# Pooled features times group weights: three fp32r matmuls a group replaced by one plain fp32 matmul

## The chip, the cores and the metric

The kernel runs on one core of a Trainium2 chip. The metric is the device time of the whole program in microseconds (us), the median of several runs. A change of the time is read against the program before.

## The reference

The program computes one layer of a decoder trunk for 2048 prompt tokens and 64 sample tokens (8 sequences of 8), with a model width of 1024. Cut to what matters:

```python
h = rmsnorm(x, g_pre_mix)
q, k, v, u = split(h @ w_in)              # 512, 128, 128, 512 columns
attn = sink_attention(rope(q), rope(k), v)  # window 128, 8 heads, 2 kv heads
# pooling: 512 channels in 4 groups of 128, windows 2, 4, 8, 16
for g, w in enumerate((2, 4, 8, 16)):
    r = trailing_mean(u[:, g], w) - u[:, g]          # (tokens, 128)
    outs.append(r @ pool_w[g])                       # pool_w[g]: (128, 128)
pooled = concat(outs) * pool_scale
x = x + rmsnorm(concat(rmsnorm(attn), rmsnorm(pooled)) @ w_out)
x = x + rmsnorm(square(relu(rmsnorm(x) @ w_up)) @ w_down)
x = x + sigmoid(x @ w_ple_gate + b_ple_gate) * (p @ w_ple)
```

All inputs and outputs are float32. The change is in the product `r @ pool_w[g]` alone.

## The kernel before

The kernel keeps float32 accuracy with fp32r matmuls: an operand is split into a high part (a cast to fp32r) and a low part (the float32 value minus the high part), and `mm3` (L136 to L140) adds three products: high by high, high by low, low by high. `lo_of` (L134) makes the low part on VectorE.

The program is a chain of stages. The first one, up to about 425 us of the profile, goes through 17 tiles: tile -1 holds the 64 sample tokens, tiles 0 to 15 hold 128 prompt tokens each. Four generators make the work of a tile:

- `front(t)`: three gemms of the transposed input `hT` with `w_in`, eight chunks of the contraction by three matmuls each. `kvps` holds keys and values (256 columns), `qps` the queries (512), `ups` the pooling input u (512). Behind them come rotation (`rope`, VectorE and GpSimd, tiles `kr`, `qr`, `rb`) and the splits `khl`, `qhl`, which TensorE turns (`trk`, `trq`) into `kp`, `qT`.
- `attention(t)`: scores in `sc` (16 matmuls), a fused mask and maximum on VectorE (L514, into `pr` and `nm`), the exponential on ScalarE, the scaling of `pr` (L540, L542), 16 transposes `trp`, their split `pt`, and the product with the values, `po`; `part` and `mix` (L565, L566) collect it.
- `pooling(t)`: four transposes of u (`tru`) into `ux`, four levels of running sums on GpSimd (`us`), the pooled features `r` on VectorE (L607), their split `rr` (L620 and L134), and the product with the group weights, `pq` (L625): 4 groups of 3 matmuls with 128 moved columns (64 for tile -1). ScalarE copies `pq` into `mix` and squares it into `sq`.
- `finish(t)`: the sum of squares over channels by a plain fp32 matmul (`pss`, L637), and the store of `mix` to DRAM (`mixd`).

The group weights are loaded once by `load_pool_w`, multiplied by the scale (L335) and split into `pw` (L336 and L134). The attention of the sample tile (`scs`, `trps`, `pos`) uses plain fp32 matmuls.

`weave` writes the generators of neighbouring tiles into each other by fixed strings (`ORDER`, `ORDERW`, `ORDER1`, `ORDER2`); a planner then orders the instructions of each engine by a model of their times, so that an edit in one place moves rows in others. On the chip each engine works through its rows in that order. When the front of tile 15 has ended, its memory is given to the next stage, `Mixed`: weights `wo` and rows `mr` are loaded, `mr` is split into `ms` (ScalarE and L134), and the products `pab` begin, woven into the last tiles' attention. From there on the program goes through the mixing product, the feed-forward part and the gate.

The PSUM pools of the first stage are `scp` (scores), `tr` (transposes), `op` (`po`, `pq`, `pss`) and `mmp` (gemms), two buffers each.

Of the kernel before, what the change touches and what calls it, by code (L numbers as in the profile page):

```python
# [10 lines left out]
F32 = mybir.dt.float32  # L11
F32R = mybir.dt.float32r
BF16 = mybir.dt.bfloat16
AF = mybir.ActivationFunctionType
ALU = mybir.AluOpType
PSUM = bass.MemoryType.PSUM

P = 128
# [40 lines left out]
def tn(t):  # L59
    return NS if t < 0 else P  # L60
# [32 lines left out]
def trunk(ctx: ExitStack, tc: tile.TileContext, i: dict, o: dict):  # L93
    nc = tc.nc
    V, A, G, T, SY = nc.vector, nc.scalar, nc.gpsimd, nc.tensor, nc.sync
# [37 lines left out]
    def lo_of(out, full, hi, eng=V):  # L133
        eng.tensor_tensor(out=out, in0=full, in1=hi.bitcast(F32), op=ALU.subtract)  # L134

    def mm3(ps, lhs, rhs, first, last):  # L136

        T.matmul(ps, lhs[0], rhs[0], start=first, stop=False)  # L138
        T.matmul(ps, lhs[0], rhs[1], start=False, stop=False)  # L139
        T.matmul(ps, lhs[1], rhs[0], start=False, stop=last)  # L140
# [138 lines left out]
    with ExitStack() as sa:  # L279

        sw = sa.enter_context(ExitStack())
        wp = sw.enter_context(tc.tile_pool(name="wp", bufs=1, reuse_waits="tile"))
        fp = sw.enter_context(tc.tile_pool(name="fp", bufs=2, reuse_waits="tile"))
        ca = sa.enter_context(tc.tile_pool(name="ca", bufs=1, side="right", reuse_waits="tile"))
        pa = sa.enter_context(tc.tile_pool(name="pa", bufs=2, side="right", reuse_waits="tile"))
        scp = sa.enter_context(tc.tile_pool(name="scp", bufs=2, space=PSUM))
        tr = sa.enter_context(tc.tile_pool(name="tr", bufs=2, space=PSUM))
        op = sa.enter_context(tc.tile_pool(name="op", bufs=2, space=PSUM))
        mmp = sw.enter_context(tc.tile_pool(name="mmp", bufs=2, space=PSUM))

        queue(gains, i["gains_t"])

# [22 lines left out]
            V.tensor_scalar_mul(nssink, ssink, -1.0)  # L315

        wi = [wp.tile([P, 2, INC], F32R, name=f"wi{k}") for k in range(8)]
        pw = ca.tile([P, 2, 4, P], F32R, name="pw")

        def load_w_in(k, part):  # L320

# [8 lines left out]
        def load_pool_w():  # L330
            raw, sc = (over.pool.tile([P, 512], F32, tag="raw", bufs=9, name="raw", padded_shape=[P, 768]) for _ in range(2))
            pr = raw.rearrange("p (g d) -> p g d", g=4)
            SY.dma_start(pr, i["pool_w"][0].rearrange("g c d -> c g d"))
            SY.dma_start(sc, i["pool_scale"].to_broadcast([P, 512]))
            V.tensor_tensor(out=pr, in0=pr, in1=sc.rearrange("p (g d) -> p g d", g=4), op=ALU.mult)  # L335
            A.copy(out=pw[:, 0], in_=pr)  # L336
            lo_of(pw[:, 1], pr, pw[:, 0])

        vps = []
        for r in range(4):  # L340
# [230 lines left out]
        def pooling(t, u, mix, sq):  # L571

            n = tn(t)
            nb, w = (NDEC, TDEC) if t < 0 else (1, P)
            L = HALO + w
            ux = pa.tile([P, 4, nb, L], F32, tag="ux", bufs=2, name="ux", padded_shape=[P, 4, nb, 184 // nb])
            if t < 0:
                G.tensor_copy(ux[:, :, :, :HALO], past["u"].rearrange("p g (b j) -> p g b j", b=nb))
            elif t == 0:
                V.memset(ux[:, :, :, :HALO], 0.0)  # L580
            else:
                V.tensor_copy(ux[:, :, :, :HALO], state["ux"][:, :, :, P : P + HALO])
            ps = tr.tile([P, 4, P], F32, tag="tr", name="tru")
            for g in range(4):
                T.transpose(ps[:, g, :n], u[:n, g * P : (g + 1) * P], ident[:n, :n])
            A.copy(out=ux[:, :, :, HALO:], in_=ps[:, :, :n].rearrange("p g (b w) -> p g b w", b=nb))
            if t >= 0:
                state["ux"] = ux
            us = pa.tile([P, 2, 4, nb, L], F32, tag="us", bufs=1, name="us", padded_shape=[P, 2, 4, nb, 184 // nb])

            def m(ap, gs, a, b):
                v = ap[:, gs, :, a:b]
                return v.rearrange("p g b l -> p (g b) l") if nb > 1 else v[:, :, 0, :]

            for lev in range(4):
                d = 1 << lev
                src = ux if lev == 0 else us[:, (lev - 1) % 2]
                gs = slice(lev, 4)
                lo = 2 * d - 1
                G.tensor_tensor(  # L600
                    out=m(us[:, lev % 2], gs, lo, L), in0=m(src, gs, lo, L), in1=m(src, gs, lo - d, L - d), op=ALU.add
                )
            yield
            r = pa.tile([P, 4, P], F32, tag="r", bufs=1, name="r")
            for lev in range(4):
                s = us[:, lev % 2, lev]
                V.scalar_tensor_tensor(  # L607
                    out=r[:, lev, :n].rearrange("p (b w) -> p b w", b=nb),
                    in0=s[:, :, HALO:],
                    scalar=1.0 / (2 << lev),  # L610
                    in1=ux[:, lev, :, HALO:],
                    op0=ALU.mult,
                    op1=ALU.subtract,
                )
                if t == 0:
                    ic = ct[:, C_ICNT + lev * 16 : C_ICNT + (lev + 1) * 16]
                    V.tensor_tensor(out=r[:, lev, :16], in0=s[:, 0, HALO : HALO + 16], in1=ic, op=ALU.mult)
                    V.tensor_tensor(out=r[:, lev, :16], in0=r[:, lev, :16], in1=ux[:, lev, 0, HALO : HALO + 16], op=ALU.subtract)
            rr = pa.tile([P, 2, 4, P], F32R, tag="rr", bufs=1, name="rr")
            V.tensor_copy(rr[:, 0, :, :n], r[:, :, :n])  # L620
            lo_of(rr[:, 1, :, :n], r[:, :, :n], rr[:, 0, :, :n])
            yield
            pq = op.tile([P, 4, P], F32, tag="o", name="pq")
            for g in range(4):
                mm3(pq[:, g, :n], (pw[:, 0, g], pw[:, 1, g]), (rr[:, 0, g, :n], rr[:, 1, g, :n]), True, True)  # L625
            A.copy(out=mix[:, 4:8, :n], in_=pq[:, :, :n])
            A.activation(out=sq[:, 4:8, :n], in_=pq[:, :, :n], func=AF.Square)

# [155 lines left out]
        run(front(-1, *heads[-1], res[-1]))  # L784
        split_head(0)
        load_pool_w()

        last = iter(())
        for t in range(-1, NT):
            kr, vr, qr, u, kp, qT = res[t]  # L790
            if t + 1 < NT and t >= 0:
                split_head(t + 1)
            mix = pa.tile([P, 8, P], F32, tag="mix", bufs=2, name="mix")
            sq = pa.tile([P, 8, P], F32, tag="sq", bufs=2, name="sq")
            if t + 2 < NT:
                heads[t + 2] = head(t + 2)
            f = front(t + 1, *heads[t + 1], res[t + 1]) if t + 1 < NT else iter(())
            p = pooling(t, u, mix, sq)
            if t < 0:
                a = sample_attention(kr, vr, qr, mix, sq)  # L800
                for c in ORDER0.split():
                    next({"a": a, "p": p, "f": f}[c], None)
                run(a, p, finish(t, mix, sq))
                over_s.__exit__(None, None, None)
                over.pool = sa.enter_context(tc.tile_pool(name="over_p", bufs=1, side="right", reuse_waits="tile"))
                run(f)
            else:
                e = split_w_out((t - 3) % 4, (t - 3) // 4) if 3 <= t < 11 else iter(())
                if t == NT - 1:
                    sw.close()  # L810
                    s2 = ctx.enter_context(ExitStack())
                    mixed = Mixed(s2)
                    bank = sw.enter_context(tc.tile_pool(name="first", bufs=2, space=PSUM, reuse_waits="tile"))
                    e = mixed.first(bank)
                order = {NT - 2: ORDER1, NT - 1: ORDER2}.get(t, ORDERW if 3 <= t < 11 else ORDER)
                weave(order, a=attention(t, kp, qT, mix, sq), p=p, f=f, l=last, e=e)
                last = finish(t, mix, sq)
# [1094 lines left out]
```

## Time and profile before

| | |
|---|---|
| three runs | 2139.48, 2139.55, 2140.86 us; median 2139.55 |
| profiled execution | 2142.09 us, its span 2140.3 us |
| mean granted TensorE clock | 0.996 |
| TensorE busy, whole span | 2113.1 us (99%) |
| VectorE busy, whole span | 1622.4 us (76%) |
| product `pq`: rows of L138, L139, L140 | 68 each, median 273 to 275 ns |
| first and last product row | 51.8 and 419.0 us |

The span is the time from the first to the last instruction; the profiled execution's own time has 1.8 us around it and lies 2.5 us above the median of the runs. TensorE's busy time includes overlap of one matmul with the next, so that a busy engine alone does not tell how dense its work is: the distance between the starts of neighbouring rows does. PE is TensorE, PEld its weight loads, DVE VectorE, ACT ScalarE, POOL GpSimd, and SP issues the DMAs.

### The profile page before, as it was taken

The numbers are of one execution on the slowest core, as the hardware profiler recorded it, in microseconds if no ns is written. First come the engines' busy times: TensorE is split into PE (matmuls) and PEld (weight loads), VectorE is DVE, ScalarE is ACT, GpSimd is POOL, SyncE is SP. The second block draws the span as 40 slices with busy tenths as digits, with TensorE's granted clock in tenths as the row PEclk, the third lists the DMA queues.
The fourth block names the chain that finished last, engine by engine and source line by source line (L and its number), as shares of the span: only waits on it lengthen the run. The fifth ranks groups of instructions, "written<-read, shape, count | busy, mean of one in ns | idle before, by whom it ended". The sixth has DMA issues, their size and how long they took to land.

```text
span 2140.3 us, 31614 instructions
## 1 busy us (share of the span) xinstructions
PE 2113.1 (99%) x11343; PEld 1863.1 (87%) x11343; DVE 1622.4 (76%) x2794; ACT 1033.0 (48%) x2019; POOL 647.8 (30%) x689
## 2 busy tenths in 40 slices
PE   8999999999999999999999999999999999999999
PEld 6888888788889999999999998888888888887787
DVE  6899888876689888755555467778888888896786
ACT  4667666544555546454554445523323323233553
POOL 2334434343451110100000004644443443432242
PEclk9999999999999999999999999999999999999999
DMA  6552222768789989986776663223123123248563
GB/s 221 177 178 84 72 62 75 266 214 234 243 245 311 310 289 339 282 258 199 223 229 202 211 206 112 79 91 122 50 91 101 50 92 101 90 154 333 188 192 124
DMA packets 334107, 379.77 MB, mean 177 GB/s; under 512 B 82239, under 2 KB 263807, under 8 KB 323678
## 3 DMA queue, kind: packets, MB, share of 16 engines
q1 hardware_dynamic: 333950, 377.76, 55.4%
q8 instruction: 89, 1.46, 0.3%
q14 instruction: 68, 0.56, 0.1%
HBM read 247.90 MB, written 131.09 MB: 177 GB/s over the span
## 4 chain that ended last, share of the span: by engine, by line
PE 79%; DVE 7%; DMA 5%; issue 3%; POOL 3%; ACT 2%; SPq 0%; ACTq 0%; POOLq 0%; DVEq 0%
PE up L1142 9%; PE up L1144 9%; PE up L1143 9%; PE dn L1426 9%; PE dn L1428 9%; PE dn L1427 9%; PE pg L1663 2%; PE pg L1665 2%; PE pg L1664 2%; PE ups L138 1%; PE ups L140 1%; PE ups L139 1%; PE qps L140 1%; PE qps L138 1%; PE qps L139 1%
## 5 line engine op out<-in xcount | busy, mean ns | idle before, releaser
L1436 DVE TENSOR_TENSOR z<-dn,z 128x512 f32<-128x512 f32 x416 | 279.6, 684 | 89.6 <-PE dn L1428 83.6
L134 DVE TENSOR_TENSOR g<-raw,g 128x512 fp32r<-128x512 f32 x336 | 234.5, 716 | 99.7 <-ACT g L211 86.2
L1142 PE MATMUL up<-e,g 128*128 128x352 f32 x832 | 268.6, 324 | 4.0 <-ACT snap L1149 3.9
L1143 PE MATMUL up<-e,g 128*128 128x352 f32 x832 | 268.0, 322 | 0.0
L1144 PE MATMUL up<-e,g 128*128 128x352 f32 x832 | 265.1, 323 | 1.2 <-DVE g L134 1.2
L211 ACT CAST g<-raw 128x512 fp32r<-128x512 f32 x336 | 203.5, 622 | 88.4 <-PE up L1144 65.6
L1375 POOL TENSOR_TENSOR raws<-raws 128x1024 f32<-128x1024 f32 x32 | 80.3, 2512 | 429.1 <-DVE r L1157 376.6
L1426 PE MATMUL dn<-wr,ms 128*128 128x512 f32 x512 | 199.3, 390 | 0.4 <-DVE z L1436 0.4
L1427 PE MATMUL dn<-wr,ms 128*128 128x512 f32 x512 | 199.2, 389 | 0.0
L1428 PE MATMUL dn<-wr,ms 128*128 128x512 f32 x512 | 198.0, 389 | 0.0
L1142 PEld LDWEIGHTS up<-e,g 128*128 128x128 f32 x832 | 156.5, 188 | 6.2 <-ACT snap L1149 5.3
L1143 PEld LDWEIGHTS up<-e,g 128*128 128x128 f32 x832 | 157.3, 189 | 0.7
L1144 PEld LDWEIGHTS up<-e,g 128*128 128x128 f32 x832 | 156.2, 189 | 1.8 <-DVE g L134 1.8
L211 ACT CAST m<-fr 128x512 fp32r<-128x512 f32 (+1 forms) x128 | 65.4, 514 | 180.7 <-PE dn L1428 154.5
L856 POOL TENSOR_TENSOR s<-fr 128x256 f32<-128x256 f32 x64 | 49.1, 767 | 333.2 <-DVE ms L134 245.1
L1426 PE MATMUL dn<-wr,m 128*128 128x512 f32 x384 | 149.7, 390 | 0.2 <-ACT zp L1484 0.2
L1428 PE MATMUL dn<-wr,m 128*128 128x512 f32 x384 | 149.5, 389 | 0.0
L1427 PE MATMUL dn<-wr,m 128*128 128x512 f32 x384 | 149.4, 389 | 0.0
L1156 DVE TENSOR_TENSOR t<-up,snap 128x352 f32<-128x352 f32 x144 | 71.3, 520 | 78.8 <-ACT snap L1149 65.9
L1149 ACT COPY snap<-up 128x352 f32<-128x352 f32 x144 | 62.2, 454 | 136.3 <-PE up L1144 136.0
L1426 PEld LDWEIGHTS dn<-wr,ms 128*128 128x128 f32 x512 | 96.1, 188 | 20.6 <-DVE z L1436 0.6
L1428 PEld LDWEIGHTS dn<-wr,ms 128*128 128x128 f32 x512 | 96.1, 188 | 20.0
(382 smaller groups left out, 5862.5 us busy)
## 6 DMA issues: line engine op xcount, KB each, us to landing
raw<-in_w_up_dram SPq DMA_DIRECT2D x160, 256.0 KB, 4.8
raw<-upt SPq DMA_DIRECT2D x32, 1024.0 KB, 8.1
fr<-ffd SPq DMA_DIRECT2D x64, 512.0 KB, 3.6
ffd<-r SPq DMA_DIRECT2D x96, 256.0 KB, 2.6
upt<-raw SPq DMA_DIRECT2D x16, 1024.0 KB, 5.2
raws<-in_w_down_dram SPq DMA_DIRECT2D x32, 512.0 KB, 5.4
sp<-hfd SPq DMA_DIRECT2D x21, 704.0 KB, 6.4
gwd<-gw SPq DMA_DIRECT2D x28, 512.0 KB, 5.4
```

The costliest lines, as they stand in the source:

```text
L134: eng.tensor_tensor(out=out, in0=full, in1=hi.bitcast(F32), op=ALU.subtract)
L211: copy(out=dst[:, 0], in_=src)
L1142: T.matmul(ps, l[0], r[0], start=st, stop=False, skip_group_check=not fresh)
L1143: T.matmul(ps, l[0], r[1], start=False, stop=False, skip_group_check=not fresh)
L1144: T.matmul(ps, l[1], r[0], start=False, stop=c == 3, skip_group_check=not fresh)
L1149: A.copy(out=s, in_=ps)
L1156: V.tensor_tensor(out=t, in0=ps, in1=s, op=ALU.add)
L1375: tc.keep_in_program_order(G.tensor_tensor(out=t, in0=x, in1=y, op=ALU.subtract))
L1426: T.matmul(ps, l[0], r[0], start=fresh and j == 0, stop=False, skip_group_check=not fresh)
L1427: T.matmul(ps, l[0], r[1], start=False, stop=False, skip_group_check=not fresh)
L1428: T.matmul(ps, l[1], r[0], start=False, stop=j == 1, skip_group_check=not fresh)
L1436: V.tensor_tensor(out=z, in0=ps, in1=z, op=ALU.add)
```

## The change

The group weights are kept as one float32 tile `pw`, written by the product with the scale itself. The pooled features `r` are not split. Each group's product is one plain fp32 matmul. The four PSUM pools of the stage are given the rule `reuse_waits="tile"`, which the other pools have already.

```diff
-        scp = sa.enter_context(tc.tile_pool(name="scp", bufs=2, space=PSUM))
-        tr = sa.enter_context(tc.tile_pool(name="tr", bufs=2, space=PSUM))
-        op = sa.enter_context(tc.tile_pool(name="op", bufs=2, space=PSUM))
-        mmp = sw.enter_context(tc.tile_pool(name="mmp", bufs=2, space=PSUM))
+        scp = sa.enter_context(tc.tile_pool(name="scp", bufs=2, space=PSUM, reuse_waits="tile"))
+        tr = sa.enter_context(tc.tile_pool(name="tr", bufs=2, space=PSUM, reuse_waits="tile"))
+        op = sa.enter_context(tc.tile_pool(name="op", bufs=2, space=PSUM, reuse_waits="tile"))
+        mmp = sw.enter_context(tc.tile_pool(name="mmp", bufs=2, space=PSUM, reuse_waits="tile"))
...
-        pw = ca.tile([P, 2, 4, P], F32R, name="pw")
+        pw = ca.tile([P, 4, P], F32, name="pw")
...
-            V.tensor_tensor(out=pr, in0=pr, in1=sc.rearrange("p (g d) -> p g d", g=4), op=ALU.mult)
-            A.copy(out=pw[:, 0], in_=pr)
-            lo_of(pw[:, 1], pr, pw[:, 0])
+            V.tensor_tensor(out=pw, in0=pr, in1=sc.rearrange("p (g d) -> p g d", g=4), op=ALU.mult)
...
-            rr = pa.tile([P, 2, 4, P], F32R, tag="rr", bufs=1, name="rr")
-            V.tensor_copy(rr[:, 0, :, :n], r[:, :, :n])
-            lo_of(rr[:, 1, :, :n], r[:, :, :n], rr[:, 0, :, :n])
             yield
             pq = op.tile([P, 4, P], F32, tag="o", name="pq")
             for g in range(4):
-                mm3(pq[:, g, :n], (pw[:, 0, g], pw[:, 1, g]), (rr[:, 0, g, :n], rr[:, 1, g, :n]), True, True)
+                T.matmul(pq[:, g, :n], pw[:, g], r[:, g, :n], start=True, stop=True)
```

Behind the edit the code's lines stand up to five lines higher, so L625 becomes L620, L562 becomes L560, and so on. The rule on the PSUM pools changes no row's place on any engine and none of its waits; the rows move by the other edits.

The first place is TensorE's order at the product of tile 6, in the middle of the stage. `vp_136` and `vp_138` are the values of two key blocks, `wi_131` and `wi_132` the last two chunks of `w_in`. Before:

```order
L563 MATMUL po<-pt,vp_138 128x512
L475 MATMUL trq<-identr,qhl 128x128 x4
L138 MATMUL pq<-rr,pw 128x128
L140 MATMUL qps<-wi_131,hT 128x512
L138 MATMUL qps<-wi_132,hT 128x512
L139 MATMUL qps<-wi_132,hT 128x512
L140 MATMUL qps<-wi_132,hT 128x512
L139 MATMUL pq<-rr,pw 128x128
```

After the change, the same product:

```order
L560 MATMUL po<-pt,vp_136 128x512
L620 MATMUL pq<-r,pw 128x128 x2
L561 MATMUL po<-pt,vp_136 128x512
L560 MATMUL po<-pt,vp_138 128x512
L561 MATMUL po<-pt,vp_138 128x512
L473 MATMUL trq<-identr,qhl 128x128 x8
L620 MATMUL pq<-r,pw 128x128 x2
L138 MATMUL ups<-wi_129,hT 128x512
```

Before, ten more rows of the product follow; the product stands at the end of the query gemm. After, it stands inside the gemm for u, the next one of the front: the front is half a gemm and more further ahead of the pooling.

The second place is TensorE's order behind the front of tile 15, the last gemm of the stage, up to the first `pab`. Before, the part where TensorE waits (24 score matmuls stand behind the last gemm row in all, 32 `trp`, 8 `trq`):

```order
L511 MATMUL sc<-kp,qT 128x256
L585 MATMUL tru<-ident,u 128x128 x4
L552 MATMUL trp<-ident,pr 128x128 x8
L464 MATMUL trk<-identr,khl 128x128 x4
L475 MATMUL trq<-identr,qhl 128x128 x8
L552 MATMUL trp<-ident,pr 128x128
L510 MATMUL sc<-kp,qT 128x256
```

After (32 score matmuls, 40 `trp` and 16 `trq` behind the last gemm row), the end of this part:

```order
L561 MATMUL po<-pt,vp_136 128x512
L550 MATMUL trp<-ident,pr 128x128 x8
L462 MATMUL trk<-identr,khl 128x128 x4
L632 MATMUL pss<-small,sq 128x1 x2
L560 MATMUL po<-pt,vp_136 128x512
L561 MATMUL po<-pt,vp_136 128x512
L560 MATMUL po<-pt,vp_138 128x512
L473 MATMUL trq<-identr,qhl 128x128 x4
L561 MATMUL po<-pt,vp_138 128x512
L473 MATMUL trq<-identr,qhl 128x128 x4
L138 MATMUL pab<-wo,ms 128x512
```

The first `pab` now comes ahead of the last tile's scores, and more of the attention stands behind the front.

The third place is VectorE's order ahead of the first split of mixed rows (`ms`), between the last rotation of queries and `ms`. Before, the last of 71 instructions:

```order
L134 TENSOR_TENSOR pt<-trp,pt 128x512
L566 TENSOR_TENSOR mix<-po,part 64x512
L537 RECIPROCAL es<-es 128x4
L514 ISA pr,nm<-sc,ct,nsink 128x256
L514 ISA nm 128x1
L134 TENSOR_TENSOR ms<-mr,ms 128x1024
```

After, the last of 53:

```order
L605 SCALAR_TENSOR_TENSOR r<-us,ux 128x128
L134 TENSOR_TENSOR pt<-trp,pt 128x512
L605 SCALAR_TENSOR_TENSOR r<-us,ux 128x128
L134 TENSOR_TENSOR pt<-trp,pt 128x512
L634 TENSOR_SCALAR ss_4922<-pss 128x2
L134 TENSOR_TENSOR ms<-mr,ms 128x1024
```

The split has moved ahead of eight score reductions of the last tile, and the `rr` rows are gone.

## Prediction

> **What bounds the kernel now.** I read the page first for the share of each engine, then a table of stretches to find the bound of the stage that the change touches, then the waits of TensorE, and last the timeline of single instructions for prices. From the page, busy time by engine; from the table of stretches, its heading and four stretches (matmul, weight load, VectorE, ScalarE, GpSimd, then the granted clock, the DMA share and GB/s):
>
> ```profile
> PE 2113.1 (99%) x11343; PEld 1863.1 (87%) x11343; DVE 1622.4 (76%) x2794; ACT 1033.0 (48%) x2019; POOL 647.8 (30%) x689
> ...
> core 0: us, PE busy (x) PEld busy (x) DVE busy (x) ACT busy (x) POOL busy (x), PEclk, DMA share, GB/s
> 36.00:40.00 4.00, 4.00 (x12) 3.18 (x12) 3.53 (x15) 3.57 (x11) 2.75 (x6) 0.59 0.41 105
> ...
> 224.00:248.00 24.00, 24.00 (x151) 21.26 (x150) 22.91 (x65) 16.27 (x44) 9.00 (x12) 1.00 0.23 70
> ...
> 392.00:400.00 8.00, 6.32 (x41) 5.84 (x40) 7.17 (x23) 6.25 (x20) 4.02 (x6) 0.79 1.02 426
> 400.00:408.00 8.00, 7.17 (x41) 5.95 (x40) 7.91 (x19) 6.77 (x18) 4.00 (x4) 1.00 1.00 370
> ```
>
> The change lives in the first stage (0 to about 425 us). Its middle has TensorE busy 24.00 of 24.00 us at full clock, VectorE at 22.9. "Busy" is modelled at the end of a matmul, so I asked for the waits. TensorE's whole list between 60 and 440 us has six rows, first and last here, 4.9 us in all:
>
> ```profile
> PE trk L464 <- DVE pt L134: 1.3, 1, 1.3
> ...
> PE po L563 <- DVE pt L134: 0.4, 2, 0.2
> ```
>
> Every one but 0.2 us of these falls after 385 us. So from 60 to 385 us TensorE is fed without a break, and a microsecond of TensorE's work removed there is a microsecond of the program. Behind the stage the next one carries on with the same engine full, so what is gained is kept. Between 385 and 415 us it is otherwise: there VectorE is full and TensorE waits for it. These are the first matmul rows behind a wait, one early and five late (start, length, what, and in brackets the idle time and its releaser):
>
> ```profile
> 42.20 0.30 PE L721 MATMUL trps<-ident,prs 128*128 128x128 f32 x1 [0.67 <-DVE prs L717]
> ...
> 389.69 0.66 PE L552 MATMUL trp<-ident,pr 128*128 128x128 f32 x4 [0.71 <-ACT ux L586]
> 391.68 0.54 PE L464 MATMUL trk<-identr,khl 128*128 128x128 f32 x4 [1.34 <-DVE pt L134]
> 392.88 0.88 PE L475 MATMUL trq<-identr,qhl 128*128 128x128 f32 x8 [0.66 <-DVE pt L134]
> 394.79 0.45 PE L552 MATMUL trp<-ident,pr 128*128 128x128 f32 x1 [1.02 <-DVE pr L542]
> ...
> 404.94 0.50 PE L140 MATMUL pab<-wo,ms 128*128 128x512 f32 x1 [0.83 <-DVE ms L134]
> ```
>
> **The change, part by part: TensorE.** Removed are 12 fp32r matmuls a tile, three for each of four groups. A busy time does not tell what one of them costs, because they overlap; the distance from start to start does. One tile's product from its third matmul to the next gemm row, and for comparison two neighbours of 256 moved columns:
>
> ```profile
> 196.71 0.28 PE L140 MATMUL pq<-rr,pw 128*128 128x128 f32 x1
> ...
> 197.71 0.27 PE L140 MATMUL pq<-rr,pw 128*128 128x128 f32 x1
> 197.82 0.45 PE L140 MATMUL ups<-wi,hT 128*128 128x512 f32 x1
> ...
> 186.02 0.28 PE L139 MATMUL kvps<-wi,hT 128*128 128x256 f32 x1
> 186.14 0.28 PE L140 MATMUL kvps<-wi,hT 128*128 128x256 f32 x1
> ```
>
> Ten steps in 197.82 - 196.71 = 1.11 us: 0.111 us each, 12 x 0.111 = 1.33 us a tile. That is as much as a matmul of twice the columns nearly (186.14 - 186.02 = 0.12), so these short ones are held by their weight loads and not by the columns they move.
>
> Added are 4 plain fp32 matmuls a tile. The trace has plain fp32 only in the sample group's attention and in the sum of squares, never in this shape. Rows from there, and one fp32r row of 512 columns:
>
> ```profile
> L730 PE MATMUL pos<-ptn,vr x4: 376/402/427, 48.6 to 50.5; 64*64 64x256 f32 x4
> L733 PE MATMUL pos<-pts,sv x32: 222/223/243, 49.2 to 51.7; 128*64 128x32 f32 x32
> ...
> 179.07 0.40 PE L140 MATMUL ups<-wi,hT 128*128 128x512 f32 x1
> ...
> 32.59 0.43 PE L689 MATMUL scs<-kn,qTs 64*128 64x64 f32 x2
> 32.95 0.42 PE L682 MATMUL scs<-kT,qTs 64*32 64x128 f32 x8
> ```
>
> L733 issues 16 matmuls and stands in the trace 32 times, so one plain fp32 matmul is two records. L730 moves 256 columns and one record of it takes 376 to 427 ns, as an fp32r matmul of 512 does (0.40 us, row of 179.07): a record streams its columns twice. At 128 columns a record should then cost what 256 fp32r columns cost, 0.12 us, and a matmul 2 x 0.12 = 0.24. Below, it cannot go under two weight loads, 2 x 0.111 = 0.22. Above, the worst row is the lone L689, 32.95 - 32.59 = 0.36 us from its start to the next row's, an idle load queue included. I take 0.24, since the new ones stand in a dense stream like the kvps rows: 4 x 0.24 = 0.96 us a tile. Gain 1.33 - 0.96 = 0.37 us a tile (ends: 0.44 at 0.22; at 0.36 a loss of 0.11). Sixteen prompt tiles: 5.9 us. The sample tile moves 64 columns, so both kinds are held by loads: 12 x 0.111 - 8 x 0.111 = 0.44 us. TensorE together: 6.4 us, with ends of 7.5 and of -1.7 (16 x -0.11).
>
> The Trainium skill (TensorE: Matmul & The Clock Gate, Back-to-back issue gap) has a sustained 81 ns for a stream of load and matmul at 128 columns. By that the old product would be 12 x 81 = 0.97 us, as dear as the new one, and the sum would lose its main term. Here the same pair takes 0.111 us over ten steps, so the measurement decides against it.
>
> **VectorE and ScalarE.** The split of the pooled features into high and low goes, as does that of the group weights; the product with the scale stays, one row as before. Groups that write rr and pw (count, then ns least/median/most):
>
> ```profile
> L620 DVE CAST rr<-r x17: 275/418/1409, 46.2 to 410.4; 128x512 fp32r<-128x512 f32 x16, 128x256 fp32r<-128x256 f32 x1
> L134 DVE TENSOR_TENSOR rr<-r,rr x17: 404/683/1193, 47.1 to 412.9; 128x512 fp32r<-128x512 f32 x16, 128x256 fp32r<-128x256 f32 x1
> L336 ACT CAST pw<-raw x1: 617/617/617, 34.2 to 34.2; 128x512 fp32r<-128x512 f32 x1
> L134 DVE TENSOR_TENSOR pw<-raw,pw x1: 1327/1327/1327, 36.0 to 36.0; 128x512 fp32r<-128x512 f32 x1
> ```
>
> That is 17 x (0.42 + 0.68) = 18.7 us of VectorE. In the middle of the stage it is worth nothing, since TensorE, full there, covers VectorE. The weights' 1.33 us at 36.0 stands in VectorE's queue ahead of the softmax scaling (L717) that the transpose at 42.20 waits for: with it gone I take that wait as gone, 0.7 us (between 0, if the rotated queries ahead of it are late anyway, and 0.8 with the restart).
>
> What is late next: the pooled features r have one buffer and are now read by TensorE itself, where before VectorE copied them at once. VectorE's r of the next tile therefore waits for the product of this one, and behind it in VectorE's queue are exponent sums and the splits of probabilities. Even at the crowded end of the stage the trace has some 5 us from a product's last row to the next tile's r:
>
> ```profile
> 386.60 0.27 PE L140 MATMUL pq<-rr,pw 128*128 128x128 f32 x1
> ...
> 391.55 0.47 DVE L607 SCALAR_TENSOR_TENSOR r<-us,ux 128x128 f32<-128x128 f32 x1
> ```
>
> So I cost that wait at nothing. The reuse rule named on the four PSUM pools moves no row and no wait in the orders, so it costs nothing and gains nothing.
>
> **The moved rows.** With fewer splits to wait for, the order lets the front's gemms run further ahead: the product of tile 6 stands among the u gemm's rows, not the query gemm's. At the end of the front more attention is therefore left over: behind the last ups row stand 32 score matmuls, 40 transposes of probabilities and 16 of queries, where there were 24, 32 and 8. VectorE's side of the end is this (the last rotation of queries, the first split of mixed rows, the last mix):
>
> ```profile
> 377.33 0.75 DVE L414 TENSOR_TENSOR rb<-qps,cs 128x256 f32<-128x256 f32 x2
> ...
> 403.22 1.67 DVE L134 TENSOR_TENSOR ms<-mr,ms 128x1024 fp32r<-128x1024 f32 x1
> ...
> 424.70 0.69 DVE L566 TENSOR_TENSOR mix<-po,part 64x512 f32<-64x512 f32 x1
> ```
>
> The first pab rows, which fill TensorE again, need ms. Between the last rb and ms VectorE has 26 us of work in 71 instructions; in the new order 53 (8 score reductions and a pair of rr fewer). So ms comes earlier relative to the front's end, but the trp and po rows that stand ahead of the first pab need almost all of those 53 too. TensorE has some 10 us of its own work between the front's end and the first pab in both orders, and waits for the rest in both. I take the waits of the end as unchanged, 4.6 us with the five rows above; how far they can move is the main uncertainty. No DMA is added or removed; the loads of wo follow the front's end as before, one store of mix rows slips behind four loads of w_up, and nobody in this stage reads it.
>
> **The sum.** 6.4 + 0.7 = 7.1 us. The profiled execution takes 2142.09 us (span 2140.3 and 1.8 around it), so 2135.0. The three timed runs have their median 2.5 us lower, at 2139.55, and the forecast for such a median is 2139.55 - 7.1 = 2132.4. Runs agree within about 0.1%; 0.2%, 4.3 us, is what a measurement of this kernel can tell from no change.
>
> **Rivals.**
> *The end eats it.* If VectorE sets the end of the stage, the program gains only what VectorE gains there. Now it needs 425.4 - 377.3 = 48.1 us from the last rotation to the last mix. The new order takes out two rr pairs (2.2 us) and puts in what slid behind the front, roughly the VectorE share of 8 score matmuls, 8 transposes and a pooling (8 reductions, 2 splits and the rest, about 7 us by the rows' durations), so 53, and starts some 8 us earlier: the last mix 3 us earlier than now. Gain 3 us, 2136.6. For it: VectorE 7.91 of 8 at 400 to 408. Against: pab matmuls fill TensorE during that time, and TensorE has its own 6 us less.
>
> *The price is wrong.* At 0.36 us a matmul TensorE gains nothing: -1.3 + 0.7 gives 2140.1, no change. For it only a lone row with idle in it; against it the L730 record. By the skill's 81 ns the removed rows would be worth only 0.97 us a tile and the time be 2138.6; the ten measured steps leave that no chance of its own.
>
> *The end gains.* If the shorter VectorE queue takes the waits at 389.69 to 404.94 away, the lowered clock behind them goes as well (0.79 over 8 us: 1.7 us lost). Four rows of the chain that ended last, 2.0 us, are removed work and speak for it, the first and the last here:
>
> ```profile
> 397.02 0.34 DVE rr L620
> ...
> 412.93 0.60 DVE rr L134
> ```
>
> Then 7.1 + 4.6 + 1.7 = 13.4 in full, 2126.2; I expect at most half of the two, 10.2 in all: 2129.3 and a little below.
>
> *Slower.* At the end the new order puts trp x8 of the last tile but one ahead of the first pab, and the probabilities they read stand far down VectorE's queue, about 16 us behind the last rotation, where TensorE has 7 us of its own work after the front. A wait there of over 7.1 us more than today's 4.6 decides it, some 12 us in one place, after which the clock falls to half and costs again, as it does at 36 to 40 (granted 0.59):
>
> ```profile
> 35.97 0.63 PE L138 MATMUL qps<-wi,hT 128*128 128x512 f32 x1
> 36.40 0.63 PE L139 MATMUL qps<-wi,hT 128*128 128x512 f32 x1
> ...
> 39.33 0.39 PE L140 MATMUL qps<-wi,hT 128*128 128x512 f32 x1
> 39.56 0.40 PE L138 MATMUL qps<-wi,hT 128*128 128x512 f32 x1
> ```
>
> There the gemm's rows step by 0.43 us for 3.4 us, and by 0.23 after. A wait grown from 4.6 to 13.4 us (8.8 more) and half speed once more for 3.4 us (1.7) give 2132.4 + 10.5 = 2142.9. The Trainium skill (TensorE: Matmul & The Clock Gate, Part 1: The HAM clock gate) says that the clock halves after an idle window of about 3.4 us; the trace shows slow stretches of that length, here without a long idle time ahead of them.
>
> **How the numbers follow.** Forecast as summed, 2130 to 2135.2: 0.47. The end gains: 0.14. The end eats it: 0.21. Price wrong: 0.09. Slower: 0.09. Faster by over 0.2% (below 2135.2) are the first two and 0.02 of the third, whose near edge crosses that line: 0.63. Within 0.2%, the rest of the third and the fourth: 0.28. Slower: 0.09. The range runs from 2127.5 (price 0.22, 1.1 us more, with over half of the end's waits gone) to 2139.5 (price wrong), and leaves about 0.17 out.
>
> **What would show it.** The new product's rows should step by 0.24 us a matmul, in two records each; nothing else should be on rr; 60 to 380 us should stay without TensorE waits, with the u gemm of the last tile ending 8 to 9 us earlier, of which 6 are gain and 3 slid behind; the transpose near 42 us should not wait; the waits between the front's end and the first pab should add up to 4 to 6 us. The forecast is wrong if the records step by more than 0.15 us, if waits appear in the middle of the stage, or if those of the end grow beyond 8 us.

## The result, and the profile after

The changed kernel is slower: 2153.57 us median (2150.88 to 2156.89, 4 runs) against 2139.52 (4 runs) for the kernel before on the same chip, a ratio of 1.0057 [1.0045, 1.0069] (in brackets the 95% interval), 14 us more where 7 fewer were forecast. The profiled execution took 2154.9 us, its span 2152.8 us, with a mean granted clock of 0.992 (0.996 before).

The page's row of busy times is nearly unchanged, so the time is not in more work:

```profile
PE 2111.2 (98%) x11275; PEld 1859.2 (86%) x11275; DVE 1614.4 (75%) x2759; ACT 1033.9 (48%) x2018; POOL 642.4 (30%) x689
```

The table of stretches (columns as in the prediction) has the four stretches shown of before, and three new ones that are not full:

```profile
core 0: us, PE busy (x) PEld busy (x) DVE busy (x) ACT busy (x) POOL busy (x), PEclk, DMA share, GB/s
36.00:40.00 4.00, 4.00 (x12) 3.13 (x12) 3.21 (x15) 3.43 (x11) 2.90 (x6) 0.60 0.44 117
104.00:128.00 24.00, 22.53 (x140) 19.47 (x139) 21.26 (x59) 17.16 (x44) 9.50 (x13) 1.00 0.60 192
...
176.00:200.00 24.00, 22.29 (x140) 19.36 (x139) 21.80 (x61) 15.87 (x42) 10.72 (x13) 1.00 0.23 70
224.00:248.00 24.00, 24.00 (x151) 21.13 (x150) 20.13 (x59) 16.30 (x43) 9.26 (x13) 1.00 0.22 70
...
392.00:400.00 8.00, 6.51 (x26) 5.36 (x26) 5.64 (x11) 5.04 (x9) 1.07 (x2) 0.50 1.01 405
400.00:408.00 8.00, 8.00 (x43) 6.78 (x42) 3.20 (x12) 3.25 (x8) 0.00 (x0) 0.94 0.89 292
416.00:440.00 24.00, 18.36 (x89) 15.05 (x88) 14.22 (x27) 9.16 (x18) 6.60 (x9) 0.90 0.37 119
```

At 400 to 408 us VectorE, 7.91 of 8 us busy before, is down to 3.20: it now waits, as TensorE does at 416 to 440. TensorE's whole list of waits between 60 and 440 us (what waited, for whom, us in total, times, longest) had 4.9 us before and has 16.8:

```profile
PE pss L632 <- POOL sq L628: 5.6, 1, 5.6
PE trp L550 <- DVE pr L540: 4.8, 2, 4.1
PE ups L138 <- DVE vp L435: 1.5, 1, 1.5
PE trk L462 <- DVE pt L134: 1.5, 1, 1.5
PE po L561 <- DVE pt L134: 1.4, 3, 1.0
PE trq L473 <- DVE pt L134: 1.3, 1, 1.3
PE po L560 <- ACT pt L552: 0.7, 2, 0.3
```

Where they stand, by TensorE's timeline (start, length, row, idle time and releaser): three of the seven in the middle of the stage, then the end. The early wait at 42.20 us of before is gone.

```profile
123.31 0.54 PE L473 MATMUL trq<-identr,qhl 128*128 128x128 f32 x4 [1.34 <-DVE pt L134]
...
171.88 0.50 PE L561 MATMUL po<-pt,vp 128*128 128x512 f32 x1 [0.98 <-DVE pt L134]
...
195.00 0.47 PE L138 MATMUL ups<-wi,hT 128*128 128x512 f32 x1 [1.54 <-DVE vp L435]
...
389.68 0.52 PE L550 MATMUL trp<-ident,pr 128*128 128x128 f32 x3 [4.14 <-DVE pr L540]
...
393.68 0.75 PE L462 MATMUL trk<-identr,khl 128*128 128x128 f32 x4 [1.49 <-DVE pt L134]
...
437.50 1.02 PE L632 MATMUL pss<-small,sq 128*128 128x1 f32 x4 [5.57 <-POOL sq L628]
```

The wait for `pss` ends a chain of the last tile on three engines, here from ScalarE's and GpSimd's timelines, and VectorE had stood idle for that tile's transposes:

```profile
405.08 0.69 DVE L134 TENSOR_TENSOR pt<-trp,pt 128x512 fp32r<-128x512 f32 x1 [4.80 <-ACT pt L552]
...
434.67 0.63 ACT L567 ACTIVATE sq<-mix 128x512 f32<-128x512 f32 x1 [2.58 <-DVE mix L564]
...
435.38 1.26 POOL L627 TENSOR_TENSOR sq<-sq 128x512 f32<-128x512 f32 x1 [12.46 <-ACT sq L567]
```

The orders explain it. Before, 60 of the first 96 `pab` rows stood ahead of the last tile's last `po`, so 36 rows (8 us) were left to cover the chain from `po` to `pss`, which took 4.7 us (423.55 to 428.24). Now all 96 stand ahead of it, and nothing covers the chain. The last `po` and the `pss` of before, without a wait, and the last `po` now:

```profile
423.55 0.39 PE L563 MATMUL po<-pt,vp 128*128 128x512 f32 x1
...
431.99 0.50 PE L637 MATMUL pss<-small,sq 128*128 128x1 f32 x4
```

```profile
431.54 0.40 PE L561 MATMUL po<-pt,vp 128*128 128x512 f32 x1
```

Behind the long waits TensorE runs at half clock (granted 0.50 at 392 to 400): `pab` rows 0.43 us apart, where they are 0.23 apart a microsecond later.

```profile
399.81 0.63 PE L140 MATMUL pab<-wo,ms 128*128 128x512 f32 x1
400.24 0.63 PE L138 MATMUL pab<-wo,ms 128*128 128x512 f32 x1
...
401.54 0.40 PE L139 MATMUL pab<-wo,ms 128*128 128x512 f32 x1
401.77 0.39 PE L140 MATMUL pab<-wo,ms 128*128 128x512 f32 x1
```

The product itself is cheaper than forecast: four matmuls became 136 records over 17 tiles, two each (the group of the product's rows: count, ns least/median/most, first and last start):

```profile
L620 PE MATMUL pq<-r,pw x136: 270/275/345, 51.3 to 425.2; 128*128 128x128 f32 x128, 128*128 128x64 f32 x8
```

By the timeline four records ahead of a gemm row take 199.80 - 199.37 = 0.43 us, 0.11 each:

```profile
199.37 0.68 PE L620 MATMUL pq<-r,pw 128*128 128x128 f32 x4
199.80 0.47 PE L139 MATMUL ups<-wi,hT 128*128 128x512 f32 x1
```

Still the last u gemm row of tile 15 starts 6.2 us earlier than before (378.3 against 384.5 us), and the last product row 6.2 us later (425.2 against 419.0).

### The profile page after: what moved, and what is told of

It is laid out like the page before. It is cut to its first block, busy times and chain, and to the rows that moved or that the text cites. A ratio compares the mean times of both kernels' runs of the same rounds, so it can differ in the third digit from the quotient of the medians.

```text
span 2152.8 us, 31431 instructions
## 1 busy us (share of the span) xinstructions
PE 2111.2 (98%) x11275; PEld 1859.2 (86%) x11275; DVE 1614.4 (75%) x2759; ACT 1033.9 (48%) x2018; POOL 642.4 (30%) x689
## 4 chain that ended last, share of the span: by engine, by line
PE 79%; DVE 7%; DMA 5%; issue 3%; POOL 3%; ACT 2%; SPq 0%; ACTq 0%; DVEq 0%; POOLq 0%
PE dn L1421 9%; PE dn L1423 9%; PE dn L1422 9%; PE up L1137 9%; PE up L1139 9%; PE up L1138 9%; PE pg L1658 2%; PE pg L1660 2%; PE pg L1659 2%; DMA sp<-hfd 1%; PE ups L138 1%; PE ups L139 1%; PE ups L140 1%; PE qps L138 1%; PE qps L140 1%
```

## The experiments

The leading theory: the new product gains what TensorE saves, and the rows that the planner moved lose three times that. The experiments hold rows in a chosen order by edges that set the issue order on one engine and add no wait. Orders are given in words below, in place of the tables `ROWS`. All were timed against the kernel before on their own chip; ratios compare these. "97th pab" is the start of that row in the profiled execution, the point where the mixing stage has left the first one behind (held kernel before: 434.1).

| run | ratio to the kernel before | 97th pab, us | span, us |
|---|---|---|---|
| kernel before, order held | 1.0004 [0.9993, 1.0014] | 434.1 | 2142.8 |
| changed kernel | 1.0057 [1.0045, 1.0069] | 438.4 | 2152.8 |
| new product, old order | 0.9990 [0.9979, 1.0000] | 422.1 | 2138.3 |
| old product, new order | 1.0110 [1.0096, 1.0124] | 447.6 | 2158.4 |
| new order to tile 11, then old | 1.0012 [1.0002, 1.0023] | 432.3 | 2145.7 |
| old to tile 11, then new | 1.0049 [1.0037, 1.0061] | 435.0 | 2150.1 |
| old to tile 15, then new | 1.0034 [1.0023, 1.0045] | 433.0 | 2147.6 |
| old to the first pab, then new | 1.0023 [1.0012, 1.0034] | 431.9 | 2146.9 |
| 96 pab rows held behind attention | 1.0017 [1.0008, 1.0025] | 431.5 | 2143.3 |
| front rows held as well | 0.9996 [0.9988, 1.0005] | 424.8 | 2138.8 |
| product three times, old order | 1.0119 [1.0100, 1.0139] | 456.0 | 2167.2 |
| u gemm shorter, old order | 0.9939 [0.9926, 0.9953] | 417.1 | 2130.4 |
| copy ahead of cast, old order | 0.9991 [0.9980, 1.0001] | 422.9 | 2137.8 |
| loads ahead of store, old order | 0.9983 [0.9974, 0.9992] | 421.8 | 2135.4 |

**The new product in the old order.** `ROWS` holds every engine's rows of the kernel before, as runs of their places in the code.

```diff
+def keep_order(tc, nc):
...
+        for p, q in zip(seq, seq[1:]):
+            tc.add_manual_dep(
+                q,
+                p.name,
+                mybir.DependencyInfo(mybir.DependencyClass.NoSync, mybir.DependencyReason.DATA),
+                reason="keep_order",
+            )
...
         trunk(tc, ins, outs)
+        keep_order(tc, nc)
```

> The changed kernel's program, with every engine's rows held in the order that they have in the kernel before (edges of issue order alone, no wait added; the four matmuls stand where the first of each group's three stood). Theory A, the planner's moved rows cost and the product itself gains: 17 x (12 x 0.111 - 8 x 0.111) = 7.5 us off 2139.5, so 2132 us; no TensorE wait over 1 us between 104 and 200 us, the last tile's finish as late against its own rows as before. Theory B, the product itself makes the waits (TensorE now reads the one buffer of r, so VectorE's next tile waits for it): at least 2150 us in the old order too. Theory C, a gain on TensorE ahead of the end is given back at the end whatever the order: about 2139.5 us.

Measured 2139.07 us median, 0.9990: 14 us better than the changed kernel, so theory B falls, and the order is shown to cost what the changed kernel lost. The number is the one that theory C names, not the 2132 us of theory A; the next runs part these two. TensorE's waits between 60 and 440 us are down to six of 3.9 us, the longest two here:

```profile
PE trk L462 <- DVE pt L134: 1.3, 1, 1.3
PE trp L550 <- ACT ux L584: 0.7, 1, 0.7
```

But the 7.5 us do not show at the end as theory A has it: the mixing stage is 10 to 12 us ahead at the 97th pab (422.1 against 432.4 and 434.1 in the two profiles of the old program), and the median 0.9 us lower than that of the kernel before, by the interval 0 to 4.5. Not all of that lead is the product's: 3.2 and 4.9 us of it stand already at 59 us, where both profiles of the old program have half clock (granted 0.66 at 35 to 40 us, 0.79 and 0.57 at 52 to 60) and this one has none. The 7.1 us by which it grows from there are what 16 tiles should give, 16 x 4 x 0.111. Why less than that shows at the end is taken up below.

**The old product in the new order.** The kernel before, `ROWS` from the changed kernel, the rows that only it has (`rr`, the further `pq`) beside their neighbours.

```diff
         trunk(tc, ins, outs)
+        keep_order(tc, nc)  # ROWS: the changed kernel's order
```

> The converse: the kernel before, with its split features, split weights and twelve fp32r matmuls a tile, but every other row of all five engines in the order that the changed kernel has. Theory A: the 14 us that the changed kernel lost and the 7.5 us that its product gained, so 2139.5 + 21.6 = about 2161 us. Theory B: the order is harmless, 2139.5 us. Theory C: between 2150 and 2154 us, since TensorE's longer product would lie in the waits.

Measured 1.0110, 24 us more than the kernel before, where theory A says 21.6, theory B none and theory C 10 to 15. The two long waits are those of the changed kernel:

```profile
PE trp L552 <- DVE pr L542: 4.1, 2, 3.8
...
PE pss L637 <- POOL sq L633: 5.6, 1, 5.6
```

With the same order, the new product is 0.53% (11 us) faster than the old one.

**New order first, old order later, and the reverse.**

```diff
-ROWS = old order
+ROWS = new order up to the last ups row of tile 11, then old order
```

> The changed program in its own (new) order up to the end of tile 11's u gemm, about 300 us, and from there in the old order. By theory A with the losses added up where the two traces show them: only the waits of the middle (104 to 200 us, 6.5 us) stay, 2132 + 6.5 = 2138.5 us. If the end's order is the whole loss (the middle's waits made good by an earlier front): 2132 us. If the early lead of the front is what brings the end out of step: 2150 us or more.

```diff
-ROWS = old order
+ROWS = old order up to the last ups row of tile 11, then new order
```

> The changed program in the old order up to the end of tile 11's u gemm, about 300 us, and from there in its own new order. By theory A with losses added up: the end (389 to 442 us, about 12 us more of waiting and half clock than before) and the entry to the up stage (about 3.7 us) stay, so 2132 + 15 = 2147 us. If the middle is the whole loss: 2132 us.

Measured 1.0012 and 1.0049. Above the new product in the old order (0.9990) the middle costs 0.22%, 5 us, and the end 0.59%, 13 us; both together cost the changed kernel 0.67%, 14 us. The sum of the two is 0.81%, 17 us, and the difference lies within the intervals. The sizes were forecast at 6.5 and 15.

**The end cut later.** Two further places of the cut.

```diff
-ROWS = old order
+ROWS = old order up to the last ups row of tile 15, then new order
```

> The changed program in the old order to the end of the last u gemm (tile 15), about 376 us, then in its new order. If the end is lost because the front runs ahead of the attention between tiles 12 and 15: the 12 us are gone, about 2139 us. If it is the rows after the last u gemm (the attention's last rows standing behind the first rows of the mixing stage): 2150 us, as with the new order from tile 11.

```diff
-ROWS = old order
+ROWS = old order up to the first pab row, then new order
```

> The changed program in the old order up to the first matmul of the mixing stage, then in its new order. It parts the two waits of the end. If both come from rows ahead of that matmul (eight transposes of the last tile but one, and what they leave late): 2139 us. If the second wait, 5.6 us of pss for the squares of the last tile, comes from where the last tile's attention stands against the first rows of the mixing stage, only the first (4.1 us for pr, and the half clock behind it) is gone: about 2144 to 2146 us. If it is the order of the mixing stage itself: 2149 us.

Measured 1.0034 and 1.0023. That the front runs ahead between tiles 12 and 15 is not what loses most of the end: held there, 0.44 of the 0.59% stays. Held up to the first `pab`, the wait for `pr` is 1.0 us, and the wait for `pss` is the only one of over 2 us:

```profile
PE pss L632 <- POOL sq L628: 5.6, 1, 5.6
...
PE trp L550 <- DVE pr L540: 1.0, 1, 1.0
```

So more than half of the end's loss by the medians, 0.33 of 0.59%, comes from rows behind the first `pab`.

**Only TensorE's rows.** All holding so far moved thousands of rows. Here TensorE alone is held, at two places, and the planner orders the rest. The expectations set two readings against each other: by reading 1 the order of TensorE's rows makes the loss, by reading 2 it stays with TensorE's order held, and so comes from the other engines' rows.

```diff
+def issue_behind(tc, nc, edges):
+    rows = [x for x in nc.cur_bb.bb.instructions if x.engine.name == "PE"]
+    for late, early in edges:
+        tc.add_manual_dep(rows[late], rows[early].name, ...)
...
         trunk(tc, ins, outs)
+        issue_behind(tc, nc, [...])  # 96 pab rows, each behind one of six trp or po rows
```

> The changed kernel with the planner's own order, but each of the first 96 matmuls of the mixing stage is issued behind the transpose or weighted value of the last two tiles' attention behind which it stood in the kernel before (six such rows; edges of issue order alone, on TensorE alone). By reading 1 the end's 10 to 13 us are gone and the middle's loss stays: 2153.6 - 12 = about 2142 us, no wait for pss, and the wait of trp for pr under 1 us. By reading 2: still about 2150 us, with the wait for pss or one of the same length for VectorE.

Measured 1.0017 against 1.0057: 0.4%, 8.6 us, where about 12 were expected, from edges on 96 rows of one engine. The planner answered them with some other rows: by the trace, 69 of VectorE's 2759 rows, 57 of ScalarE's and 12 of GpSimd's stand at another place than in the changed kernel. The wait for `pss` is gone from the list. The expectation missed that the wait for `pr` would stay: it comes from rows ahead of the first `pab`, and is still the longest one:

```profile
PE trp L550 <- DVE pr L540: 4.4, 2, 4.1
PE po L561 <- DVE pt L134: 1.7, 4, 1.1
PE ups L138 <- DVE vp L435: 1.5, 1, 1.5
```

```diff
+        issue_behind(tc, nc, [...])  # also kvps, qps, ups and pq rows, behind the trp or po row they followed
```

> The same, and in every tile the front's matmuls (kvps, qps, ups) and the pooled product are issued behind the attention's transposes and weighted values behind which they stood in the kernel before; the other engines' rows are left to the planner. By reading 1 TensorE's waits between 104 and 200 us are gone as well: the time of the new product in the old order, 2139 us (no slower than the kernel before). By reading 2: the middle's 6.5 us stay, 2145 us or more.

Measured 0.9996, the time of the kernel before and 0.06% from the whole old order; of the waits between 104 and 200 us one of 1.2 us is left. This is what reading 1 forecast: edges on TensorE that put the front's and the mixing stage's matmuls back behind the attention's are enough to take the loss away. They do not show that the other engines' rows have no part in it, for the planner moved those too: 767 of VectorE's 2759 rows stand at another place than in the changed kernel, and 536 at another than in the old order (820 differ between these two). One engine's rows in the old order with all other engines held in the new one was not tried, since their rows would wait for each other.

**The price by itself.**

```diff
-                T.matmul(pq[:, g, :n], pw[:, g], r[:, g, :n], start=True, stop=True)
+                for _ in range(3):
+                    T.matmul(pq[:, g, :n], pw[:, g], r[:, g, :n], start=True, stop=True)
```

> New product in the old order, but each of the four fp32 matmuls is issued three times into the same place (each starts afresh, so the output does not change). It prices the matmul alone: 17 x 8 more matmuls, 136. At 0.22 us each 30 us more than the new product in the old order, about 2169 us by the median and 30 us later at the first row of the mixing stage. At the 0.24 us of the prediction 33 us; at the upper bound of 0.36 us 49 us. If arriving early is paid back later (a stage paced by transfers), arriving 30 us late gives that back: the end moves by 4 to 8 us less than the first row of the mixing stage.

Eighteen records to the next gemm row take 254.07 - 252.07 = 2.00 us, 0.111 us a record and 0.22 a matmul:

```profile
252.07 2.24 PE L621 MATMUL pq<-r,pw 128*128 128x128 f32 x18
254.07 0.49 PE L139 MATMUL qps<-wi,hT 128*128 128x512 f32 x1
```

The median is 2167.04, 1.29% above the new product in the old order, 27.6 us; 136 x 0.22 = 30. The 97th pab came 34 us later than in the new product in the old order, 4 of them there already at the first row of the product (54.9 against 50.6 us). From there to the end 6 us were given back at most.

**Where the rest of the gain goes.** First the control, which prices the holding itself.

```diff
         trunk(tc, ins, outs)
+        keep_order(tc, nc)  # in the kernel before, ROWS: its own order
```

> A control: the kernel before, every row of every engine held in the order it already has. If holding the order costs nothing, 2140 us as the kernel before on this chip, and the same stage times as the kernel before (mixing stage begins at 401.4 us of the span, up stage at 607.1). If holding costs something, it is slower by that, and the gain of the new product in the old order is larger than was measured by the same amount.

Measured 1.0004: holding costs nothing that can be told.

```diff
-                    mm3(
+                    if c0 == 768 and k in (1, 2, 3):
+                        ...  # high by high and high by low alone
+                        continue
+                    mm3(
```

> New product in the old order, and of the u gemm's 24 matmuls of 512 columns a tile three are left out (the low part of the weight against the high part of hT, in three of eight row groups): 17 x 3 x 0.227 = 11.6 us less TensorE time in the first stage. It asks where the new product's 7.5 us went in the old order, of which the median showed 1 us. If time won in the first stage is carried on and the loss was scatter of a run: 2139 - 11.6 = 2127.5 us. If transfers behind the first stage set a floor (the mixing stage and the first loads of the up stage), which the kernel before just reaches and an earlier arrival runs into: the first row of the mixing stage 11 us earlier still, the end between 2135 and 2139 us, and the excess in TensorE's waits between 500 and 760 us.

This kernel leaves out the low part of `hT` by the high part of `w_in` in three of eight chunks (the expectation names the two parts the other way round). Measured 0.9939, 0.51% (11 us) below the new product in the old order, for 11.6 us of matmuls left out. The profiles show less: the 97th `pab` comes 5.0 us earlier (417.1 against 422.1), since TensorE's waits between 60 and 440 us grew from 3.9 to 8.0 us, and the span ends 7.9 us earlier. So not all that was left out became time, but what had been won at the 97th `pab` reached the end. A floor behind the first stage, as the expectation had it for the second case, does not show.

```diff
-ROWS = old order
+ROWS = old order, snap<-up ahead of l<-sp on ScalarE
```

> New product in the old order with one row moved on ScalarE: the first copy snap<-up of the up stage stands ahead of the cast l<-sp, which waits for a load of 704 KB. In the new product in the old order TensorE waits 4.3 us there for that copy and then runs some 12 matmuls at half clock (0.295 instead of 0.160 us a step, 1.6 us). If that wait is where the early lead goes: 4 to 6 us faster than the new product in the old order, about 2134 us, and faster than the kernel before by 0.2% or more. If the stage is paced by the transfers, TensorE waits a few rows later for l instead, and the time is 2139 us again.

Measured 0.9991, no gain. In the new product in the old order TensorE waited 4.3 us for the copy at the entry of the up stage (first row). The kernel before waits there too, 3.1 and 4.1 us in its two profiles, so this wait is little of what the new one loses against it. With the copy moved TensorE waits for the weights instead (second row):

```profile
PE up L1137 <- ACT snap L1144: 4.5, 2, 4.3
```

```profile
PE up L1137 <- ACT g L211: 4.8, 2, 3.0
```

```diff
-ROWS = old order, snap<-up ahead of l<-sp on ScalarE
+ROWS = the same, and x1d<-xt behind four raw<-in_w_up and one sp<-hfd on SP's queue
```

> New product in the old order with two rows moved at the entry of the up stage: the copy snap<-up ahead of the cast l<-sp on ScalarE, as before, and on SP's queue one store x1d<-xt, which waits 3.3 us for VectorE with four loads of w_up and one of sp behind it, moved behind these five loads. If the entry waits because those loads are issued late: they go out 3 us earlier, the 4.8 us of waits for the cast g and the half clock behind them shrink by 3 to 5 us, so about 2135 us. If the transfers themselves are the limit there (the DMA engines are busy at 0.99 to 1.0 from 600 us on): no gain, 2139 us.

Measured 0.9983 [0.9974, 0.9992], 2138.07 us against 2141.47: the one version here that computes everything and is faster than both kernels by its whole interval, by 3.6 us. Against the copy alone (0.9991) the intervals overlap. SP's queue shows that moving the loads 3 us ahead brings them little: the four then take 6.87 us to be issued, where they took 2.97 in the new product in the old order. The DMA engines were full meanwhile (share 1.06 at 598 to 605 us); that this is the reason is not shown.

```profile
598.55 6.87 SPq L1092 DMA_DIRECT2D raw<-in_w_up_dram  x4
605.52 0.66 SPq L993 DMA_DIRECT2D sp<-hfd  x1
606.22 0.43 SPq L881 DMA_DIRECT2D x1d<-xt  x1
```

What stays open is why a lead of 10 to 12 us at the 97th pab is 0 to 5.6 us at the end in the kernels with the new product held in the old order. Their profiles have more short waits of TensorE behind 430 us: the rows' gaps of over 0.25 us add up to 10.6 and 11.5 us in the two profiles of the old program, and to 17.3, 16.2 and 14.1 us in those of the new product in the old order, of the copy ahead of the cast and of the loads ahead of the store. They lie in the mixing stage (for `z`), at the entry of the up stage and at weight rows, 0.4 to 2.1 us each, and nothing was found that joins them. Row by row against the held kernel before, whose TensorE rows stand in the same order from there on, the lead of the new product in the old order is 12.0 us at the 97th `pab`, 9.8 behind the wait for `z` (554 us), 8.5 at 623 us, 7.2 at 667, 6.0 at 850 and 4.3 at the end: it is lost in steps of 0.4 to 2.2 us, most of it by 670 us. These are single profiled executions; the two of the old program end 2.5 us apart.

## Why the prediction was wrong, point by point

- **The price.** Right in kind, two records a matmul, and a little mis-sized: 0.22 us a matmul, the lower bound, not 0.24. The estimate by 256 streamed columns was too high; a record steps like the short fp32r matmul, 0.111 us. TensorE's gain is 17 x 4 x 0.111 = 7.5 us, not 6.4. The lower end of the sum, -1.7, leaves out the sample tile's 0.44; with it the end is -1.3, as the rival has it. The two orders, each with both products, put it at 0.14% (3 us, old order, not clear of nothing by the intervals) and 0.53% (11 us, new order) at the end of the program.
- **VectorE's rr rows, worth nothing in the middle.** Nothing speaks against it: in the old order TensorE's lead from 59 us on is the product's own 7.1 us. That TensorE now reads r costs nothing that shows: in the old order no wait of its list has to do with r.
- **The wait of 42.20 gone.** It is gone, but by luck: the reason given, the split of the weights ahead of it in VectorE's queue, is wrong. In the old order, with the split left out, TensorE still waits 0.67 us there (at 41.03), and the old product in the new order, with the split kept, has no wait there. It is the order that removes it.
- **"60 to 380 us should stay without TensorE waits."** Wrong. Seven waits of 4.9 us stand between 123 and 195 us. The prediction had seen that the front runs half a gemm further ahead and weighed this at the end alone. Five of the waits are of `po` for `pt`, one is of `trq` and one of the front itself for the split of the values (`vp`, 1.54 us). That the front's lead takes rows away that had covered the attention's chain from `trp` over ScalarE and VectorE to `po` is read from the orders; the middle's share, by the order alone, is 0.22%, 5 us.
- **"I take the waits of the end as unchanged, 4.6 us."** This is the step that failed most: 4.14 + 0.66 + 1.49 + 5.57 = 11.9 us in the rows of 389.68 to 437.50, and half clock twice, where it came once before (0.79 at 392 to 400). Up to the first `pab`, where the prediction looked, they are 6.3 us; the other 5.57, for `pss`, come behind it, where it put no wait at all. Held in the old order up to tile 11, the end alone costs 0.59%, 13 us.
- **The rival "slower".** Its mechanism was there, as described: the eight `trp` of the last tile but one wait 4.14 us for probabilities, half clock follows. It was priced too low, at 2142.9 us against 2153.6. Two reasons show. It looked only at rows ahead of the first `pab`, while the larger part came behind it, where all 96 `pab` rows go ahead of the last tile's `po`. And the prediction counted on VectorE's shorter queue, 53 instructions for 71 (as relief in *The end gains*); that does not help when VectorE itself waits for transposes that TensorE has put off (4.80 us idle at 405.08).
- **"What is gained is kept."** Partly wrong, also in the old order: of the product's 7.5 us the median shows 0 to 4.5, and where the rest goes stays open. With the u gemm shortened as well the further lead at the 97th `pab` was kept to the end.
- **The rivals "the end eats it" and "the end gains"** took the old order's end with other lengths. Neither is what happened, since its rows were others.

## What to carry to other kernels

Where a planner sets the order by modelled times, an edit is two changes, the work and the order, and here the order weighed twice as much as the work. Read the new order for what no longer covers a chain: count the rows of the busy engine that stand between the last matmul of a chain and the row that waits for its result, and ask what is left when they have moved ahead. Hold the old order with edges of issue order to price the work alone; 96 such edges at the place of the loss gave back 8.6 of 14 us.

## What the runs showed of the hardware

A plain fp32 matmul of 128 by 128 weights and 128 moved columns costs 0.22 us in a dense stream, two records of 0.111 us each, as much as two fp32r matmuls of that size and no more. In the changed kernel, between 60 and 440 us, half clock followed the long waits and none of the short ones: 1.54 us at 195.00 and 1.34 us at 123.31 left the steps as they were, 4.14 us at 389.68 and 5.57 us at 437.50 did not (0.50 granted at 392 to 400, 0.51 at 435 to 442). The Trainium skill (TensorE: Matmul & The Clock Gate, Part 1: The HAM clock gate) puts the loss of the clock at an idle window of about 3.4 us; these four waits agree with it. Others here do not: in the kernel before, three waits of 0.71, 1.34 and 0.66 us between 389 and 393 us were enough (0.57 granted at 394 to 398), and in the old product in the new order a single one of 1.88 us at 149.79, with 0.57 granted at 152 to 156.
